# Sums over partitions and the spreading of 1/rms in the layer norms: two fp32r parts instead of float32

## The chip, the cores and the metric

The kernel runs on one core of a Trainium2 chip. The core has five engines that work side by side, each through its own queue in order: TensorE (PE, matrix products; PEld is its weight load), VectorE (DVE), ScalarE (ACT), GpSimd (POOL) and SyncE (SP, which issues the DMAs). The metric is the device time of one execution in microseconds (us). The kernel before took 1206.88 us, the median of three runs from 1206.43 to 1207.32.

## The reference

The program is a decoder trunk of two layers for one sequence of 512 tokens with 1024 features. What matters here is that each layer has three RMS norms over the features, and that every one feeds a matrix product:

```python
def rms_norm(x, g):
    y = x * lax.rsqrt(jnp.mean(x * x, axis=-1, keepdims=True) + EPS)
    return y * g
for l in range(DEPTH):
    hn = rms_norm(h, g_mix[l]);  proj = hn @ w_in[l]
    # causal differential attention (4 heads) and a gated recurrent block on proj
    h = h + jnp.concatenate([o, y], axis=-1) @ w_out[l]
    hm = rms_norm(h, g_mlp[l]);  h = h + jnp.square(jax.nn.relu(hm @ w_mlp_in[l])) @ w_mlp_out[l]
    gate = jax.nn.sigmoid(rms_norm(h, g_ple[l]) @ w_ple_gate[l])
    h = h + gate * (p[l] @ w_ple_proj[l])
return rms_norm(h, g_final)
```

## The kernel before

**Layout.** Features lie on the 128 partitions, tokens along the free dimension: `h` is eight tiles of 128x512. A product of a weight chunk (`wh`, `wl`) with activations (`hgh`, `hgl`, or `ffh`, `ffl`) fills an accumulator of 128x512. Each factor is cut into two fp32r parts, a rounded one (`...h`, ScalarE copy) and the rest (`...l`, VectorE subtraction); `split` (L506) does both. Each product then is three fp32r products (`mm3`, L511): high by high, high by low, low by high.

**Norms.** Nothing waits for 1/rms before a product: the weights are applied to `h` times the gain, and the accumulator is multiplied by 1/rms afterwards. `Norm.tile` (L671 on) squares each tile of `h` on ScalarE and adds it to `acc` on VectorE. `Norm.stats` (L692) sums `acc` over the partitions on TensorE: for each of four blocks of 128 tokens one float32 product with a column of 1/1024 (`onesd`), into `msq`, so that the tokens now lie on the partitions; then `me` (VectorE adds epsilon) and `rT` (GpSimd takes the power -1/2; at the feed-forward norm, which needs 1/ms, VectorE takes a reciprocal). `Norm.spread` (L706) brings it back with four float32 products: the stationary factor is a column of `rT`, repeated 128 times, and the moving one the identity (`ident`), into `bc`; ScalarE copies that to `rbc`. Everything that reads `rbc` evicts an accumulator: `xp`, `grx` and the rotary factors `cr`, `sr` (mix norm), `dn` (feed-forward norm), `gt` (embedding norm). There are six such norms, mix, feed-forward and embedding in each of two layers. The norm at the end is a class of its own (`FinalNorm`), and the norm of the heads calls the free function `spread` (L710).

**Accumulators.** `PM` (L419) draws from a ring of six banks for `dense`, `pj`, `up`, `pv` and `sc`; a seventh accumulator waits until the first reader is done with its bank. `PS` has two banks, for `msq`, `bc` and the small ones.

**Embedding stage.** `ple` (L1183) takes two tiles of features at a time: `pj` (the embedding's projection, 2 x 6 products) and then two `dense` (the gate, 48 products). In the first call of a layer all but the last of eight parts are done ahead, then `stats` and `spread` are recorded, then the rest (`late=1`, `mid=ple_ready`, L1225). `gate_done` reads `dense` and `rbc` into `gt`. The mix norm stands in the same way between the parts of the first two `dense` groups of a layer (`norm_ready`, L852).

**Order.** Nothing is issued as it is recorded. A planner (`Plan.schedule`, L184) simulates all engines with a table of costs (`Plan.cost`, L105), picks the next instruction within a window of 600 and also assigns buffers; the instructions are then issued in its order. On TensorE it counts for a float32 product four times its columns and at least 4 x 128, and for an fp32r product its columns and at least 256 (L114).

Of the kernel before, what the change touches and what calls it, by code (L numbers as in the profile page):

```python
# [11 lines left out]
F32 = mybir.dt.float32  # L12
F32R = mybir.dt.float32r
I32 = mybir.dt.int32
AF = mybir.ActivationFunctionType
ALU = mybir.AluOpType
# [3 lines left out]
NT = S // 128  # L20
D = 1024
# [8 lines left out]
EPS = 1e-6  # L30
# [370 lines left out]
def build(ctx: ExitStack, tc: tile.TileContext, given, x, p, pos, w, vec, lamqk, out):  # L401
    rnc = tc.nc
    nc = Plan(rnc, WIN, ('raw', 'wh', 'wl'), given)
    act = nc.scalar.activation
    ve = nc.vector
    mm = nc.tensor.matmul

    const = ctx.enter_context(tc.tile_pool(name="const", bufs=1))
# [7 lines left out]
    def T(name, dt=F32, n=S):  # L416
        return nc.tile(tp, [128, n], dt, "t", TB, name)
# [4 lines left out]
    def PS(name):  # L422
        return nc.tile(pss, [128, S], F32, "ps", 2, name)

    def SM(name, n, dt=F32):
        return nc.tile(small, [128, n], dt, name, 4, name)
# [79 lines left out]
    def split(src, hi, lo):  # L506

        act(out=hi, in_=src, func=AF.Copy)
        ve.tensor_tensor(out=lo, in0=src, in1=hi.bitcast(F32), op=ALU.subtract)
# [12 lines left out]
    identr = const.tile([128, 128], F32R, name="identr")  # L522
    maskr = const.tile([128, 128], F32R, name="maskr")
    onesd = const.tile([128, 1], F32, name="onesd")
    onese = const.tile([128, 1], F32, name="onese")
    mhalf = const.tile([128, 16], F32, name="mhalf")
    hb = const.tile([128, DEPTH, 8], F32, name="hb")
# [22 lines left out]
    def const_setup():  # L550
        make_identity(rnc, ident)
        ve.tensor_copy(out=identr, in_=ident)
        mk = T("mk")[:, 0:128]
        make_causal_mask(rnc, mk, mask_val=-1e30)
        ve.tensor_copy(out=maskr, in_=mk)
        nc.gpsimd.memset(onesd, 1.0 / D)
        nc.gpsimd.memset(onese, 1.0 / 128)
        nc.gpsimd.memset(mhalf, -0.5)

# [111 lines left out]
    class Norm:  # L671
# [20 lines left out]
        def stats(self, square=False):  # L692

            ps = PS("msq")
            for j in range(NT):
                mm(ps[:, j:j + 1], lhsT=self.acc[:, j * 128:(j + 1) * 128], rhs=onesd, start=True, stop=True)
            me = SM("me", NT)
            ve.tensor_scalar(out=me, in0=ps[:, 0:NT], scalar1=EPS, scalar2=None, op0=ALU.add)
            r = SM("rT", NT)
            if square:  # L700
                ve.reciprocal(out=r, in_=me)
            else:
                nc.gpsimd.tensor_tensor(out=r, in0=me, in1=mhalf[:, 0:NT], op=ALU.pow)
            self.rT = r

        def spread(self):  # L706
            self.bc = T("rbc")
            spread(self.rT, 0, self.bc)

    def spread(r, c, dst):  # L710
        ps = PS("bc")
# [66 lines left out]
    def layer(l, h, nm, last):  # L778
# [227 lines left out]
        def head_out(hd):  # L1006
            o, r = ho.pop(hd)
            ps = spread(r, 0, None)
            ve.tensor_tensor(out=o, in0=o, in1=ps, op=ALU.mult)
            hi, lo = T("oh", F32R), T("ol", F32R)  # L1010
            split(o, hi, lo)
            yo[hd] = (hi, lo)
# [222 lines left out]
    with tc.manual_schedule():  # L1235
# [3 lines left out]
        posi = T("posi", I32)[:, 0:NT]  # L1239
        split(*halves[0])  # L1240
        const_setup()
        nm = Norm("g_mix", 0)
        h = []
        for m in range(KD):
            t = T("h")
# [24 lines left out]
def trunk(tc, x, p, pos, w, vec, lamqk, out):  # L1270
    import concourse.bacc as bacc
    nc = bacc.Bacc("TRN2", target_bir_lowering=False, num_devices=1)
    a = [nc.dram_tensor(f"a{i}", t.shape, t.dtype, kind="ExternalInput").ap() for i, t in enumerate((x, p, pos, w, vec, lamqk, out))]
    with tile.TileContext(nc) as t0:
        plan = build(t0, None, *a)
    build(tc, plan, x, p, pos, w, vec, lamqk, out)
# [64 lines left out]
```

## Time and profile before

| | us |
|---|---|
| median of three runs (range) | 1206.88 (1206.43 to 1207.32) |
| the profiled execution | 1207.2 |
| its span, first to last instruction | 1205.2 |
| TensorE busy | 1191.3 (99%) |
| VectorE busy | 947.6 (79%) |
| ScalarE busy | 664.3 (55%) |
| GpSimd busy | 19.8 (2%) |
| share of TensorE in the chain that ended last | 91% |

The profiled execution took 2.0 us more than its span. An engine's busy time is the union of its instructions' times. Since TensorE's products overlap each other, the record of one is longer than its share: the distance from the start of one to the start of the next is its real cost. TensorE's granted clock is 0.996 of full speed over the span. Most of the kernel's instructions carry the line of the helper that issues them (L182), so rows are told apart by the names of the tiles, written out<-in.

### The profile page before, as it was taken

To read this page: it belongs to the slowest core of one execution; us is meant where nothing else is said; L and a number is where in the kernel's file an instruction comes from. 1 tells how busy PE (TensorE), PEld (TensorE's weight loads), DVE (VectorE), ACT (ScalarE), POOL (GpSimd) and SP (SyncE) were. 2 spreads that over 40 slices of the span, in tenths; PEclk is the share of its full clock that TensorE was granted. 3 is DMA by queue.
4 is the path that set the end of the run, shared out by engine and by line. 5 is a ranking of instruction groups with operands and counts; after the bars stand their busy time and mean duration, and the time that the engine had idled before them with its cause. 6 is when DMAs were issued, how large, how long until landed. Compare 5 with 4: busy or idle time off the path is not lost.

```text
span 1205.2 us, 17677 instructions
## 1 busy us (share of the span) xinstructions
PE 1191.3 (99%) x6848; PEld 1048.2 (87%) x6848; DVE 947.6 (79%) x1642; ACT 664.3 (55%) x1084; POOL 19.8 (2%) x43
## 2 busy tenths in 40 slices
PE   9999999999999999999999999999999999999996
PEld 6888888988989989988888888899899898898896
DVE  9899989987777678575778999799786787776564
ACT  6878747643534535543458777476355254364352
POOL 1000000000000000000000000000000000000000
PEclk9999999999999999999999999999999999999998
DMA  6321132243333333332323212224332333343202
GB/s 238 105 70 53 36 123 88 88 144 101 106 106 90 103 105 109 101 106 89 104 71 106 69 36 70 88 88 134 95 106 88 105 106 106 93 125 98 88 1 70
DMA packets 34371, 114.71 MB, mean 95 GB/s; under 512 B 3952, under 2 KB 6000, under 8 KB 34288
## 3 DMA queue, kind: packets, MB, share of 16 engines
q1 hardware_dynamic: 34288, 113.59, 30.3%
q8 instruction: 54, 0.88, 0.3%
q14 instruction: 29, 0.24, 0.1%
HBM read 111.48 MB, written 2.10 MB: 94 GB/s over the span
## 4 chain that ended last, share of the span: by engine, by line
PE 91%; DVE 5%; ACT 2%; issue 0%; DMA 0%; SPq 0%; POOLq 0%; DVEq 0%; ACTq 0%
PE dense L182 54%; PE up L182 27%; PE pv L182 2%; PE pj L182 2%; PE sc L182 2%; PE bc L182 1%; PE av L182 1%; DVE qr L182 1%; PE tr L182 1%; PE msq L182 1%; DVE wl L182 1%; DVE q L182 1%; PE osm L182 0%; PE gates L182 0%; DMA h<-x 0%
## 5 line engine op out<-in xcount | busy, mean ns | idle before, releaser
L182 ACT ACTIVATE wh<-raw 128x1024 fp32r<-128x1024 f32 x204 | 214.3, 1057 | 278.0 <-PE dense L182 154.5
L182 DVE TENSOR_TENSOR wl<-raw,wh 128x1024 fp32r<-128x1024 f32 x204 | 247.7, 1219 | 22.4 <-ACT wh L182 21.9
L182 PE MATMUL dense<-ffh,wh 128*128 128x512 f32 x512 | 199.5, 390 | 0.0
L182 PE MATMUL dense<-ffl,wh 128*128 128x512 f32 x512 | 199.3, 389 | 0.0
L182 PE MATMUL dense<-ffh,wl 128*128 128x512 f32 x512 | 199.2, 389 | 0.0
L182 PE MATMUL dense<-hgl,wh 128*128 128x512 f32 (+1 forms) x400 | 151.7, 379 | 0.0
L182 PE MATMUL dense<-hgh,wh 128*128 128x512 f32 (+1 forms) x400 | 150.8, 377 | 0.0
L182 PE MATMUL dense<-hgh,wl 128*128 128x512 f32 (+1 forms) x400 | 150.6, 376 | 0.0
L182 PEld LDWEIGHTS dense<-ffh,wl 128*128 128x128 f32 x512 | 96.1, 188 | 20.0
L182 PEld LDWEIGHTS dense<-ffh,wh 128*128 128x128 f32 x512 | 96.2, 188 | 19.7
L182 PEld LDWEIGHTS dense<-ffl,wh 128*128 128x128 f32 x512 | 96.2, 188 | 19.6
L182 DVE TENSOR_TENSOR dn<-dense,rbc 128x512 f32<-128x512 f32 x64 | 44.2, 691 | 73.5 <-PE dense L182 72.6
L182 PE MATMUL up<-bl,wh 128*128 128x256 f32 x352 | 99.6, 283 | 0.0
L182 PE MATMUL up<-bh,wl 128*128 128x256 f32 x352 | 99.6, 283 | 0.0
L182 PE MATMUL up<-bh,wh 128*128 128x256 f32 x352 | 99.5, 283 | 0.0
L182 ACT ACTIVATE sh<-s 128x512 fp32r<-128x512 f32 x96 | 60.0, 628 | 69.0 <-DVE s L182 68.2
L182 PEld LDWEIGHTS dense<-hgh,wh 128*128 128x128 f32 x400 | 75.5, 189 | 12.2
L182 PEld LDWEIGHTS dense<-hgl,wh 128*128 128x128 f32 x400 | 75.5, 189 | 11.9
L182 PEld LDWEIGHTS dense<-hgh,wl 128*128 128x128 f32 x400 | 75.5, 189 | 11.7
L182 PE MATMUL up<-bl,sh 128*128 128x256 f32 x288 | 81.5, 283 | 0.0
L182 PE MATMUL up<-bh,sl 128*128 128x256 f32 x288 | 81.5, 283 | 0.0
L182 PE MATMUL up<-bh,sh 128*128 128x256 f32 x288 | 81.4, 283 | 0.0
(237 smaller groups left out, 2576.5 us busy)
## 6 DMA issues: line engine op xcount, KB each, us to landing
raw<-w SPq DMA_DIRECT2D x204, 512.0 KB, 3.6
h<-x SPq DMA_DIRECT2D x8, 256.0 KB, 5.6
out<-fin SPq DMA_DIRECT2D x8, 256.0 KB, 2.4
w<-w SPq DMA_DIRECT2D x4, 256.0 KB, 4.5
pT<-p SPq DMA_DIRECT2D x4, 256.0 KB, 3.9
lq<-lamqk SPq DMA_DIRECT2D x1, 256.0 KB, 6.9
vt<-vec SPq DMA_DIRECT2D x1, 61.0 KB, 2.4
posi<-pos SPq DMA_DIRECT2D x1, 2.0 KB, 3.6
```

Of the source, the lines that this page charges most:

```text
L182: d["fn"](*d["args"], **d["kw"])
```

## The change

In `stats`, `acc` is split into two fp32r parts, `ach` (ScalarE) and `acl` (VectorE), and the four float32 products become eight fp32r products with two equal columns of 1/1024 (`onesr`); `me` reads every second column. In `Norm.spread`, `rT` is split on VectorE into `rh` (a cast) and `rl` (a subtraction), and the four float32 products become eight fp32r products with `identr`, an fp32r identity that the kernel already had. The final norm and the norm of the heads stay in float32.

```diff
--- before.py
+++ after.py
@@ -522,6 +522,7 @@
     identr = const.tile([128, 128], F32R, name="identr")
     maskr = const.tile([128, 128], F32R, name="maskr")
     onesd = const.tile([128, 1], F32, name="onesd")
+    onesr = const.tile([128, 2], F32R, name="onesr")
     onese = const.tile([128, 1], F32, name="onese")
     mhalf = const.tile([128, 16], F32, name="mhalf")
     hb = const.tile([128, DEPTH, 8], F32, name="hb")
@@ -554,6 +555,7 @@
         make_causal_mask(rnc, mk, mask_val=-1e30)
         ve.tensor_copy(out=maskr, in_=mk)
         nc.gpsimd.memset(onesd, 1.0 / D)
+        nc.gpsimd.memset(onesr.bitcast(F32), 1.0 / D)
         nc.gpsimd.memset(onese, 1.0 / 128)
         nc.gpsimd.memset(mhalf, -0.5)
 
@@ -692,10 +694,14 @@
         def stats(self, square=False):
 
             ps = PS("msq")
+            hi, lo = T("ach", F32R), T("acl", F32R)
+            split(self.acc, hi, lo)
             for j in range(NT):
-                mm(ps[:, j:j + 1], lhsT=self.acc[:, j * 128:(j + 1) * 128], rhs=onesd, start=True, stop=True)
+                ts = slice(j * 128, (j + 1) * 128)
+                mm(ps[:, 2 * j:2 * j + 2], lhsT=hi[:, ts], rhs=onesr, start=True, stop=False)
+                mm(ps[:, 2 * j:2 * j + 2], lhsT=lo[:, ts], rhs=onesr, start=False, stop=True)
             me = SM("me", NT)
-            ve.tensor_scalar(out=me, in0=ps[:, 0:NT], scalar1=EPS, scalar2=None, op0=ALU.add)
+            ve.tensor_scalar(out=me, in0=ps[:, 0:2 * NT].rearrange("p (j t) -> p j t", t=2)[:, :, 0], scalar1=EPS, scalar2=None, op0=ALU.add)
             r = SM("rT", NT)
             if square:
                 ve.reciprocal(out=r, in_=me)
@@ -705,7 +711,15 @@
 
         def spread(self):
             self.bc = T("rbc")
-            spread(self.rT, 0, self.bc)
+            rh, rl = SM("rh", NT, F32R), SM("rl", NT, F32R)
+            ve.tensor_copy(out=rh, in_=self.rT)
+            ve.tensor_tensor(out=rl, in0=self.rT, in1=rh.bitcast(F32), op=ALU.subtract)
+            ps = PS("bc")
+            for j in range(NT):
+                for r in (rh, rl):
+                    mm(ps[:, j * 128:(j + 1) * 128], lhsT=r[:, j:j + 1].to_broadcast([128, 128]), rhs=identr,
+                       start=r is rh, stop=r is rl)
+            act(out=self.bc, in_=ps, func=AF.Copy)
 
     def spread(r, c, dst):
         ps = PS("bc")
```

The planner then makes another order. Apart from tiles' numbers, TensorE's queue differs in layer 0 between its mix norm and the end of its attention, and from there on only within some fifty products around each norm.

TensorE, embedding norm of layer 0, before: the spreading (one row, four float32 products), ten products of the second pair's `pj`, and the first `dense` of that pair.

```order
L182 MATMUL bc_1254<-ident_77,rT_1252 128x128 x4
L182 MATMUL pj_1269<-pTh_1232,wl_1216 128x512
L182 MATMUL pj_1269<-pTh_1235,wh_1215 128x512
L182 MATMUL pj_1269<-pTl_1236,wh_1215 128x512
L182 MATMUL pj_1269<-pTh_1235,wl_1216 128x512
L182 MATMUL pj_1270<-pTh_1232,wh_1215 128x512
L182 MATMUL pj_1270<-pTl_1233,wh_1215 128x512
L182 MATMUL pj_1270<-pTh_1232,wl_1216 128x512
L182 MATMUL pj_1270<-pTh_1235,wh_1215 128x512
L182 MATMUL pj_1270<-pTl_1236,wh_1215 128x512
L182 MATMUL pj_1270<-pTh_1235,wl_1216 128x512
L182 MATMUL dense_1271<-hgh_1176,wh_1240 128x512
```

TensorE, the same place now, up to the same first `dense`; one `rh` product of the spreading stands six `pj` products further up.

```order
L182 MATMUL pj_1283<-pTh_1241,wl_1225 128x512
L182 MATMUL bc_1267<-identr_78,rl_1266 128x128
L182 MATMUL bc_1267<-identr_78,rh_1265 128x128
L182 MATMUL bc_1267<-identr_78,rl_1266 128x128
L182 MATMUL bc_1267<-identr_78,rh_1265 128x128
L182 MATMUL bc_1267<-identr_78,rl_1266 128x128
L182 MATMUL bc_1267<-identr_78,rh_1265 128x128
L182 MATMUL bc_1267<-identr_78,rl_1266 128x128
L182 MATMUL pj_1283<-pTh_1244,wh_1224 128x512
L182 MATMUL pj_1283<-pTl_1245,wh_1224 128x512
L182 MATMUL pj_1283<-pTh_1244,wl_1225 128x512
L182 MATMUL dense_1284<-hgh_1185,wh_1249 128x512
```

The last part of the spreading moved behind seven of the ten `pj` products: three stand between it and `dense`, not ten.

VectorE at the same norm, as a difference (wl is a weight chunk's low part, `gt` the first reader of `rbc`):

```order
+L182 TENSOR_TENSOR acl<-acc,ach 128x512
 L182 TENSOR_SCALAR me<-msq 128x4
-L182 TENSOR_TENSOR wl<-raw,wh 128x1024 x2
+L182 CAST rh<-rT 128x4
+L182 TENSOR_TENSOR wl<-raw,wh 128x1024
+L182 TENSOR_TENSOR rl<-rT,rh 128x4
+L182 TENSOR_TENSOR wl<-raw,wh 128x1024
 L182 TENSOR_TENSOR gt<-dense,rbc 128x512 x2
```

`acl` stands ahead of `me`; `rh` waits for GpSimd's `rT` with a `wl` behind it, and `rl` stands between two `wl`.

VectorE at the mix norm of layer 0, before, from `me` to the first reader of `rbc` (`turn`, `rd` and `sp5` belong to the set-up of rotary angles and of the recurrent block's constants):

```order
L182 TENSOR_SCALAR me_188<-msq_187 128x4
L182 TENSOR_TENSOR turn_163<-turn_163,pr_159 128x64
L182 TENSOR_TENSOR sp5_175<-sp5_175,sp4_174 128x8
L182 TENSOR_TENSOR wl_213<-raw_181,wh_212 128x1024
L182 TENSOR_TENSOR turn_163<-turn_163,pr_159 128x64
L182 TENSOR_SCALAR sp5_175<-sp5_175 128x8
L182 TENSOR_TENSOR wl_215<-raw_184,wh_214 128x1024
L182 TENSOR_SCALAR rd_164<-turn_163 128x64
L182 TENSOR_TENSOR sp5_175<-sp5_175,sp4_174 128x8
L182 TENSOR_TENSOR wl_230<-raw_216,wh_229 128x1024
L182 TENSOR_TENSOR xp_192<-dense_185,rbc_190 128x512
```

VectorE at the same norm now, from `me` to `rl`; `acl` stands six rows further up, in the place that `me` had, and `xp` nine rows further down, behind two more `wl`:

```order
L182 TENSOR_SCALAR me_191<-msq_188 128x4
L182 TENSOR_SCALAR rd_165<-turn_164 128x64
L182 TENSOR_TENSOR sp5_176<-sp5_176,sp4_175 128x8
L182 TENSOR_TENSOR wl_220<-raw_185,wh_219 128x1024
L182 TENSOR_SCALAR rd_165<-rd_165 128x64
L182 TENSOR_SCALAR sp5_176<-sp5_176 128x8
L182 CAST rh_194<-rT_192 128x4
L182 TENSOR_TENSOR turn_164<-turn_164,rd_165 128x64
L182 TENSOR_TENSOR sp5_176<-sp5_176,sp3_174 128x8
L182 TENSOR_TENSOR rl_195<-rT_192,rh_194 128x4
```

`me` moved down by six rows, `rh` and `rl` came in between it and `xp`, and the queue's small set-up work moved up between them.

## Rows read from the trace of the kernel before

**Rows 1.** The page: busy us, share, instructions; and VectorE's busy tenths in 40 slices.

```profile
PE 1191.3 (99%) x6848; PEld 1048.2 (87%) x6848; DVE 947.6 (79%) x1642; ACT 664.3 (55%) x1084; POOL 19.8 (2%) x43
...
DVE  9899989987777678575778999799786787776564
```

**Rows 2.** The chain that ended last, in time: start us, length us, engine and work.

```profile
20.49 0.79 PE msq L182 x8
...
249.51 1.39 PE dense L182 x6
...
461.70 40.31 PE up L182 x336
502.01 43.55 PE dense L182 x192
```

**Rows 3.** TensorE's waits for scores: in total us, times, longest us.

```profile
PE sc L182 <- ACT pr L182: 0.9, 2, 0.7
PE sc L182 <- ACT ky L182: 0.8, 1, 0.8
```

**Rows 4.** Timeline, embedding norm of layer 0: start us, length us, engine, work, [idle before].

```profile
557.41 0.39 PE L182 MATMUL dense<-hgh,wl 128*128 128x512 f32 x1
...
557.64 0.95 PE L182 MATMUL msq<-onesd,acc 128*128 128x1 f32 x8
...
558.45 0.49 PE L182 MATMUL dense<-hgh,wh 128*128 128x512 f32 x1
...
558.62 0.16 DVE L182 TENSOR_SCALAR me<-msq 128x4 f32<-128x4 f32 x1 [9.20 <-PE msq L182]
558.77 0.40 PE L182 MATMUL dense<-hgl,wh 128*128 128x512 f32 x1
...
558.86 1.01 POOL L182 TENSOR_TENSOR rT<-me,mhalf 128x4 f32<-128x4 f32 x1 [386.48 <-DVE me L182]
...
560.35 2.36 DVE L182 TENSOR_TENSOR wl<-raw,wh 128x1024 fp32r<-128x1024 f32 x2 [1.56 <-ACT wh L182]
...
560.39 1.05 PE L182 MATMUL bc<-ident,rT 128*128 128x128 f32 x8
...
561.20 0.47 PE L182 MATMUL pj<-pTh,wl 128*128 128x512 f32 x1
...
561.48 0.60 ACT L182 ACTIVATE rbc<-bc 128x512 f32<-128x512 f32 x1 [0.23 <-PE bc L182]
...
562.62 1.28 DVE L182 TENSOR_TENSOR gt<-dense,rbc 128x512 f32<-128x512 f32 x2
...
563.58 0.40 PE L182 MATMUL dense<-hgh,wh 128*128 128x512 f32 x1
```

**Rows 5.** Timeline of TensorE in attention of layer 0, narrow fp32r products.

```profile
118.59 0.28 PE L182 MATMUL sc<-ky,qx 128*128 128x256 f32 x1
...
118.82 0.22 PE L182 MATMUL sc<-maskr,identr 128*128 128x128 f32 x1
118.89 0.45 PE L182 MATMUL dense<-hgh,wh 128*128 128x512 f32 x1
119.17 0.49 PE L182 MATMUL tr<-ident,pr 128*128 128x128 f32 x3
```

**Rows 6.** Groups by line and shape: busy us, mean ns | idle before us.

```profile
L182 DVE TENSOR_TENSOR xcl<-xc,xch 128x512 fp32r<-128x512 f32 x8 | 5.3, 684 | 1.1 <-ACT xch L182 1.1
...
L182 ACT ACTIVATE xch<-xc 128x512 fp32r<-128x512 f32 x8 | 4.9, 622 | 0.6 <-DVE xc L182 0.5
```

**Rows 7.** Timeline, mix norm of layer 0: VectorE and GpSimd.

```profile
28.55 0.16 DVE L182 TENSOR_SCALAR me<-msq 128x4 f32<-128x4 f32 x1
...
28.86 2.07 POOL L182 TENSOR_TENSOR rT<-me,mhalf 128x4 f32<-128x4 f32 x1 [25.46 <-DVE turn L182]
...
32.81 1.29 DVE L182 TENSOR_TENSOR xp<-dense,rbc 128x512 f32<-128x512 f32 x2
```

**Rows 8.** Timeline of VectorE, first reader of layer 0's feed-forward norm.

```profile
261.11 0.68 DVE L182 TENSOR_TENSOR dn<-dense,rbc 128x512 f32<-128x512 f32 x1
```

## The prediction

> **What bounds the kernel now.** I read the page's busy shares first, then the chain that ended last in order of time, then TensorE's waits, and last the timeline around each norm. TensorE is busy 99% of the span [rows 1]. Its own spacing shows what that means: 192 products of 512 columns take 43.55 us, 0.227 us each, and 336 of 256 columns take 40.31 us, 0.120 us each [rows 2]. Such stretches follow each other with nothing between them in the feed-forward and embedding stages. So an edit shows in the time if it changes what TensorE has to stream, or makes it stand still. The exception is attention of layer 0, from about 30 to 180 us, where VectorE is busy at nine tenths or more in most slices [rows 1] and TensorE now and then waits for scores; the two listed waits there and in layer 1 come to 1.7 us [rows 3].
>
> **TensorE's own work: nothing.** There are six norms of the kind that the diff touches (mix, feed-forward and embedding, in two layers; the final one is left alone). In each, four float32 products for the sums stand in the trace as eight records, and four for the spreading as eight. Afterwards there are eight plus eight products in fp32r, one record each: 96 narrow records before, 96 after. Their price before: from the last wide product ahead of the sums to the second one behind them is 558.77 - 557.41 = 1.36 us; less two wide pitches of 0.227 that leaves 0.906 us for eight, 0.113 each. The eight of the spreading stand from 560.39 to 561.20, the same 0.81 us as the sums' from 557.64 to 558.45 [rows 4], so 0.113 too, though they have 128 columns and the sums one. The number of columns does not set that price. For fp32r there is a narrow row: the mask product of 128 columns. From 118.59 to 119.17 us stand two of 256 columns, one mask product and one wide one: 0.58 - 2 x 0.120 - 0.227 = 0.113 us [rows 5]. Same price, so 16 x 0.113 = 1.8 us per norm before and after: 0 in sum. Two columns in fp32r are not in the trace. The bounds: 0.057 (half of a narrow record; then 96 x 0.056 = 5.4 us are gained), and 0.120 (the 256-column row; then 0.7 us lost). I take 0.113, the fp32r row with the nearest shape.
>
> The Trainium skill, "TensorE: Matmul & The Clock Gate", section "Weight-path perf modes", has a fast weight load that is on when 128 weights are loaded in a type other than FP32, about twice as fast where measured; the same table says that fp32 gains nothing from it. By its trigger the change would gain, by its width not. The row of the mask product, 0.113 us in fp32r as in float32, speaks for no gain here.
>
> **What each norm's chain gains in length.** Before: sums, `me` (VectorE 0.16), `rT` (GpSimd 1.01), spreading, `rbc` (ScalarE 0.60) [rows 4]. New ahead of the sums: `ach` on ScalarE, priced as `xch` 0.62, and `acl` on VectorE, as `xcl` 0.68 [rows 6]. New between `rT` and the spreading: `rh` and `rl` on VectorE, 128x4 each, like `me` 0.16 each. That is 1.6 us of work and three more handoffs of 0.1 to 0.2 us each (from the end of `me` at 558.78 to `rT` it is 0.08; from the end of the sums at 558.45 to `me` 0.17) [rows 4]: 1.9 to 2.2 us. As load it is nothing: ScalarE +3.7 us and VectorE +6.0 us over the span, where they are busy 55% and 79% [rows 1]. What counts is who stands still for the delay, and that differs by stage.
>
> **Embedding norms (two): +1.1 us each.** VectorE idles 9.20 us ahead of `me` [rows 4], so `ach` and `acl` are done long before TensorE comes to the sums, and the sums stay where they were. But the order now puts only three `pj` products between the last spreading product and the next `dense`, where ten stood. That `dense` needs a seventh accumulator of a ring of six (two `pj` and two `dense` of the first pair, two `pj` of the second): it can start only when `gt` has read the first `dense`. Before, ten `pj` covered 561.20 to 563.58 = 2.38 us; `rbc` started 0.28 after 561.20, took 0.60, VectorE was held by two `wl` until 562.6, `gt` took 0.64, and TensorE went on at 563.58 [rows 4] with no gap. Needed without the `wl`: 0.28 + 0.60 + 0.64 and a handoff of 0.1 to 0.2 on either side of `gt`, 1.8 us. Left as cover: three `pj`, the first of which pays 0.32 like the product behind the sums, so 0.32 + 2 x 0.227 = 0.77. Short by 1.0 to 1.1 us; I take 1.1. Queued behind `rh` on VectorE are one `wl`, `rl` and another `wl`; `rl` comes at about 561.7 by the pair's 1.18 us each, and TensorE asks for it at 562.1, so that wait stays hidden. Bounds per norm: 0 if `gt` frees its bank in time, 2.0 if `gt` also queues behind a `wl`. The pattern is the same in both layers: 2.2 us.
>
> **Feed-forward norms (two): 0.** Here the order moves the sums past the end of the `up` products and the spreading 14 wide products behind the sums. `dense` began at 249.51 [rows 2] with the sums (0.9 us) ahead of it, so now at about 248.6; nine plus five plus fourteen wide products and sixteen narrow ones end at about 256.8, and `rbc` 0.9 later at 257.7. Its first reader `dn` started at 261.11 [rows 8], since it waits for its product. Some 3 us of cover remain. Bounds 0 and +0.5 (if `rl` comes late behind `ffl`).
>
> **Mix norm of layer 1: +0.3 us.** Fifteen wide products stand ahead of the last part of the spreading, instead of eight, so `xp` comes up to 7 x 0.227 = 1.6 us later. The first gate products stand 32 wide products behind the spreading instead of 35, so 0.9 us later in TensorE's queue. That is 0.7 us short; half of it I count as slack. Bounds 0 and 1.6.
>
> **Mix norm of layer 0: +1.0 us.** VectorE has no idle time here. `acl` takes the place in the queue where `me` stood at 28.55 [rows 7]; the first sum stands seven wide products behind 20.49, where the sums stood [rows 2], and the other seven 34 wide products further, so at 20.49 + 41 x 0.227 = 29.8 or a little later; `me` falls to 31, `rT` follows with 2.07 us as before, `rh` behind it holds VectorE's queue, and `xp` starts at about 35 instead of 32.81. TensorE has `pv` products to stream meanwhile. VectorE itself has 0.68 + 2 x 0.16 = 1.0 us more to do in a stretch in which it is nearly full. The order of layer 0's attention is also another one: the first scores stand earlier in TensorE's queue by some 3 us, their operands earlier on VectorE by less. The bounds: -1.7 (all waits for scores gone [rows 3]) and +3.1 (1.0 us of VectorE work and the 2.1 us of `rT` that now holds the queue, all of it TensorE's). I take +1.0, the work added to the full engine.
>
> **Sum:** 0 + 2.2 + 0 + 0.3 + 1.0 = +3.5 us. The profiled run took 1207.2 us with a span of 1205.2, so 1208.7 in the span and 1210.7 for the run. The median of the runs, 1206.88, lies 0.3 us under the profiled one: 1210.4 us.
>
> **Rivals.** *The cover holds.* The bank of the first `dense` comes free in time, as the DVE-to-TensorE handoff may be shorter and the `pj` slower, and layer 0 fills its gap with `pv`. For it: that VectorE is 79% busy and idles for 9 us ahead of `me`. Against it: seven `pj` of 0.227 less cover. Then only +0.8 us remains, 1207.7. *Layer 0 pays in full.* `rh` blocks VectorE behind the slow GpSimd `rT`, and scores come late for all four heads: 3.1 instead of 1.0 and 0.5 at one feed-forward norm: +6.1, 1213.0. For it the 9s of VectorE; against it the `pv` products, which wait for no norm. *Narrow fp32r passes are cheap* (the other side): at a price p per record the change gains 96 x (0.113 - p). It breaks even with +3.5 at p = 0.077, is faster by 0.2% at 0.051, and at 0.057 gives 1210.4 - 5.4 = 1205.0. For it: fp32r streams 256 columns at 0.120, the rate at which float32 takes 128 in two records. Against it: the mask row.
>
> This last rival is what the fast weight load of the Trainium skill's page named above would make of the time.
>
> **How the numbers follow.** 0.2% of 1206.9 is 2.4 us, about what a measurement of this kernel can tell from no change, so faster means under 1204.5 and slower over 1209.3. Forecast 0.50, of it 0.08 under 1209.3; cover holds 0.24, all of it within; layer 0 in full 0.16, slower; cheap passes 0.10, of it 0.06 faster. Slower 0.42 + 0.16 = 0.58, faster 0.06, same 0.36. The forecast's own range is 1208.5 to 1212.5; with the rivals until one fifth is left out, 1206.0 to 1214.0.
>
> **What would show it.** Right: eight sums in a row at the embedding norm still take 0.8 to 0.9 us; a gap of about 1 us on TensorE ahead of the first `dense` behind the last `pj`, released by VectorE's `gt`, in both layers; no gap in the feed-forward. Wrong: sums and spreading under 0.6 us for eight, or no gap there, or TensorE's waits in layer 0's attention changed by more than 3 us either way.

## The result, and the profile after

| | us |
|---|---|
| before, median of four runs (range) | 1206.66 (1206.31 to 1207.32) |
| after, median of four runs (range) | 1214.55 (1212.87 to 1215.72) |
| predicted | 1210.4 (1206.0 to 1214.0) |
| profiled execution after, its span | 1212.87, 1210.8 |

The ratio is 1.0064, with a 95% interval from 1.0051 to 1.0076. The kernel became slower, as forecast, but by 7.9 us instead of 3.5, and the time lies outside the range. The profiled execution is the fastest of the four, so the profiles can account for 5.7 of the 7.9 us (1212.87 less 1207.2).

TensorE's work did not change. On the page of the kernel after, the busy times answer to [rows 1]; the columns are the same.

```profile
PE 1191.9 (98%) x6848; PEld 1049.3 (87%) x6848; DVE 952.6 (79%) x1660; ACT 667.5 (55%) x1090; POOL 18.4 (2%) x44
```

TensorE is busy 1191.9 us instead of 1191.3, in a span 5.6 us longer, so 5.0 us more are spent standing still; time lost to a lower clock counts as busy. TensorE's waits answer to [rows 3]:

```profile
PE sc L182 <- ACT pr L182: 2.1, 3, 1.6
...
PE sc L182 <- ACT kl L182: 1.4, 1, 1.4
PE dense L182 <- DVE gt L182: 1.4, 2, 0.7
PE sc L182 <- ACT ky L182: 1.3, 2, 1.1
```

The waits for scores grew from 1.7 to 4.8 us; the prediction had named a change of more than 3 us there as a sign that it was wrong. The wait for `gt` is new.

The embedding norm of layer 0, to be laid beside [rows 4] (start us, length us, engine, work, [idle before]):

```profile
561.79 0.17 PE L182 MATMUL msq<-onesr,ach 128*128 128x2 f32 x1
...
562.60 0.48 PE L182 MATMUL dense<-hgh,wh 128*128 128x512 f32 x1
...
566.27 0.22 PE L182 MATMUL bc<-identr,rl 128*128 128x128 f32 x1
...
567.01 0.44 PE L182 MATMUL pj<-pTh,wh 128*128 128x512 f32 x1
...
567.21 0.60 ACT L182 ACTIVATE rbc<-bc 128x512 f32<-128x512 f32 x1 [1.80 <-PE bc L182]
...
567.51 0.40 PE L182 MATMUL pj<-pTh,wl 128*128 128x512 f32 x1
...
567.84 1.29 DVE L182 TENSOR_TENSOR gt<-dense,rbc 128x512 f32<-128x512 f32 x2 [0.92 <-ACT rbc L182]
...
568.58 0.50 PE L182 MATMUL dense<-hgh,wh 128*128 128x512 f32 x1 [0.68 <-DVE gt L182]
```

Eight sums take from 561.79 to 562.60, 0.81 us, and seven products of the spreading from 566.27 to 567.01, 0.74 us: 0.10 to 0.11 us each, as in float32. Then three `pj` products stand where ten stood, the last starts at 567.51 and would let the next product start at 567.74; `dense` starts at 568.58, released by `gt`. The wait is the forecast one.

Layer 0's attention in stretches, before and then after (TensorE busy, its weight load, VectorE, ScalarE, GpSimd busy, each with its number of instructions; then granted clock, DMA share, GB/s):

```profile
60.00:66.00 6.00, 6.00 (x28) 4.99 (x27) 6.00 (x8) 6.00 (x9) 0.00 (x0) 1.00 0.00 1
...
80.00:84.00 4.00, 3.19 (x18) 2.34 (x16) 3.94 (x7) 3.49 (x6) 0.00 (x0) 1.00 0.43 130
...
92.00:100.00 8.00, 8.00 (x40) 6.60 (x39) 7.76 (x21) 7.82 (x17) 0.00 (x0) 1.00 0.42 131
```

The same stretches after, and the one from 84 to 88 us:

```profile
60.00:66.00 6.00, 6.00 (x28) 4.99 (x27) 3.68 (x6) 5.95 (x9) 0.00 (x0) 1.00 0.00 0
...
80.00:84.00 4.00, 1.92 (x9) 1.60 (x10) 3.94 (x6) 3.88 (x6) 0.00 (x0) 0.88 0.00 0
84.00:88.00 4.00, 4.00 (x16) 3.29 (x16) 4.00 (x11) 0.56 (x1) 0.00 (x0) 0.69 0.65 230
92.00:100.00 8.00, 6.38 (x30) 5.17 (x30) 7.73 (x17) 7.00 (x16) 0.00 (x0) 1.00 0.36 96
```

Read down the columns. From 60 to 66 us TensorE loses nothing in either, but VectorE, full before, is idle for 2.3 us after. From 80 to 84 us TensorE is busy 1.92 us instead of 3.19. From 84 to 88 us it is "busy" all the time, but at a granted clock of 0.69. From 92 to 100 us it stands still again. TensorE's own rows of that stretch:

```profile
80.50 0.50 PE L182 MATMUL sc<-ky,qx 128*128 128x128 f32 x2 [1.08 <-ACT ky L182]
...
82.88 0.33 PE L182 MATMUL sc<-kl,qx 128*128 128x128 f32 x1 [1.41 <-ACT kl L182]
...
84.08 0.73 PE L182 MATMUL dense<-hgh,wl 128*128 128x512 f32 x1
84.61 0.63 PE L182 MATMUL dense<-hgh,wh 128*128 128x512 f32 x1
85.04 0.63 PE L182 MATMUL dense<-hgl,wh 128*128 128x512 f32 x1
...
86.63 0.40 PE L182 MATMUL dense<-hgh,wl 128*128 128x512 f32 x1
...
93.81 0.44 PE L182 MATMUL sc<-ky,qx 128*128 128x384 f32 x1 [1.62 <-ACT pr L182]
```

Three waits, 1.08 for `ky`, 1.41 for `kl`, 1.62 for `pr`, and between them wide products 0.43 us apart instead of 0.227. In the prediction's terms this is the step "mix norm of layer 0: +1.0". The same place before, TensorE's first score of `ky`, ScalarE's `kl`, and TensorE's first score of `kl`:

```profile
81.75 0.67 PE L182 MATMUL sc<-ky,qx 128*128 128x128 f32 x3 [0.81 <-ACT ky L182]
...
82.72 1.35 ACT L182 ACTIVATE kl<-kl 64x512 fp32r<-64x512 f32 x2 [0.36 <-DVE kl L182]
...
83.78 0.22 PE L182 MATMUL sc<-kl,qx 128*128 128x128 f32 x1
```

Before, 342 products stand ahead of the first score of `kl`, seven of them wide ones between the scores of `ky` and of `kl` (7 x 0.227 = 1.6 us). In the changed kernel 327 stand ahead, and no wide one in between. ScalarE begins `kl` 0.5 us sooner than before (82.20, in its rows further down, instead of 82.72). So the operand does not come later: TensorE asks for it sooner, and the cover is gone, as at the embedding norms.

For the comparisons below I worked out from the records how long TensorE stood still or ran slow up to a given time: the start of a product, less a full-speed pitch for every product ahead of it (0.227, 0.173, 0.120 and 0.108 us for 512, 384, 256 and at most 128 columns). The table gives what a kernel's profiled execution lost more than that of before, in two stretches and around the two embedding norms, and the difference of the medians within one comparison.

| kernel | 50 to 95 us | 95 to 180 us | embedding norms | medians | ratio, 95% interval |
|---|---|---|---|---|---|
| after | +6.3 | -1.9 | +1.0, +0.9 | +7.9 | 1.0051 to 1.0076 |
| e1 two parts in layer 0's mix norm only | +5.9 | -2.0 | 0.0, 0.0 | +4.9 | 1.0028 to 1.0053 |
| e2 in the five others only | 0.0 | -0.2 | +1.0, +1.0 | +2.2 | 1.0007 to 1.0025 |
| e3 all, old order | 0.0 | -0.1 | 0.0, 0.0 | +1.4 | 0.9999 to 1.0017 |
| e8 all, old order, split later | 0.0 | -0.2 | 0.0, 0.0 | 0.0 | 0.9991 to 1.0009 |
| e4 float32, window 580 | 0.0 | -0.7 | 0.0, 0.0 | -0.6 | 0.9985 to 1.0003 |
| e5 all, table constant 2.5 | +2.9 | +4.7 | +1.0, +0.9 | +8.1 | 1.0057 to 1.0082 |
| e14 all, window 560 | +5.8 | -1.2 | +1.0, +0.9 | +7.5 | 1.0047 to 1.0072 |
| e15 all, table constant 10 | 0.0 | -0.2 | +1.0, +0.9 | +2.6 | 1.0010 to 1.0028 |
| e7 after, two table loads fewer | +5.3 | -2.0 | +1.0, +0.9 | +5.5 | 1.0041 to 1.0068 |
| e9 after, less VectorE work | +4.9 | -2.0 | +1.0, +0.9 | +5.9 | 1.0033 to 1.0059 |
| e13 after, both | +3.3 | -2.0 | +1.0, +1.0 | +4.2 | 1.0020 to 1.0044 |
| e6 before, two table loads more | +3.0 | -0.4 | 0.0, 0.0 | +2.4 | 1.0012 to 1.0031 |
| e10 before, VectorE work at 69 us | +2.0 | 0.0 | 0.0, 0.0 | +4.5 | 1.0021 to 1.0047 |
| e11 before, the same at 30 us | 0.0 | 0.0 | 0.0, 0.0 | +0.8 | 0.9997 to 1.0015 |
| e12 old order, fewer narrow products | 0.0 | -0.1 | +0.3, +0.4 | -0.6 | 0.9985 to 1.0002 |
| e16 the same, feed-forward norms only | 0.0 | -0.2 | 0.0, 0.0 | -2.9 | 0.9968 to 0.9987 |

The -1.9 from 95 to 180 us is time that before loses there itself and the other order does not: from 120 to 150 us TensorE is busy 29.3 of 30 us before, 30.0 after. Outside these stretches no profile of a kernel with the change differs from before's by more than 0.4 us, except e12 (+0.7 at each feed-forward norm), the first 50 us, where they scatter from -0.6 to +1.1 (e3 +1.7), and the last 20 us, where before's profile loses up to 1.0 us more than theirs.

### The profile page after: what moved, and what is told of

Read it like the earlier page. It is cut to its first block, busy times and chain, and to the rows that moved or that the text cites. A ratio compares the mean times of both kernels' runs of the same rounds, so it can differ in the third digit from the quotient of the medians.

```text
span 1210.8 us, 17703 instructions
## 1 busy us (share of the span) xinstructions
PE 1191.9 (98%) x6848; PEld 1049.3 (87%) x6848; DVE 952.6 (79%) x1660; ACT 667.5 (55%) x1090; POOL 18.4 (2%) x44
## 4 chain that ended last, share of the span: by engine, by line
PE 90%; DVE 4%; ACT 4%; DMA 1%; issue 1%; SPq 0%; POOL 0%; POOLq 0%; DVEq 0%; ACTq 0%
PE dense L182 53%; PE up L182 27%; PE pv L182 3%; PE pj L182 2%; PE sc L182 2%; PE av L182 1%; PE bc L182 1%; ACT L182 1%; PE tr L182 1%; DVE wl L182 1%; PE gates L182 1%; ACT pr L182 0%; PE msq L182 0%; ACT a L182 0%; DMA raw<-w 0%
```

## Experiments: in which norm, and is it work or order

The first kernel makes the two parts in one norm, the second in the other five:

```diff
 class Norm:
+    self.two = g == "g_mix" and l == 0        # e1; in e2: not (...)
 def stats(self, square=False):
+    if self.two: ...two parts...  else: ...float32...
```

**e1.**

> Two parts only in the mix norm of layer 0; the other five norms stay in float32. Up to about 180 us the order is then the one of the changed kernel, behind it the one of before. The changed kernel lost 7.9 us by its median; in its profile TensorE lost 4.2 us more than before between 75 and 180 us and 1.0 us at each embedding norm. If the excess over the forecast lies in layer 0, as I hold: +4.2 to +6 us over before, with waits of TensorE for kl and for pr near 81 and 94 us and a lower granted clock behind them, and no wait of dense for gt. If it lay in the sum of many small costs over all six norms (rival): at most +2.

**e2.**

> Two parts in five norms; the mix norm of layer 0 stays in float32, and with it the order up to 180 us is the one of before. If the excess lies in layer 0: +2.0 us over before (two waits of dense for gt of about 1.0 each), nothing in the two feed-forward norms and in the mix norm of layer 1. Rival, costs spread over all norms: +5 or more.

Measured +4.9 and +2.2, together 7.1 of the 7.9. e2 shows the forecast's two embedding norms (2.2) to a tenth, and nothing else. e1 has nearly the whole excess (+4.9 where +1.0 was forecast), and in the same place as the changed kernel. The many-small-costs rival falls.

For the next the planner runs on the float32 program, and the new instructions are put into its order by hand:

```diff
 def issue(self):
-    for i in self.given.order:
+    old = self.given                      # plan of the float32 program
+    place(last + 1, k, "split")           # behind the last write of acc
+    place(later(sums, 24), k, "sums")     # k = 0: 24 TensorE products later
+    place(later(bc, 5), k, "bc")          # k = 0: 5 products later
+    ...
```

**e3.**

> The whole change, all six norms, but the planner runs on the float32 program: every other instruction keeps before's order and buffers, and the new ones are put in by hand, ach and acl right behind the last addition into acc, the sums and the spreading near their old places (in the mix norm of layer 0 the sums 24 and the spreading 5 products later, in the feed-forward norms 24 and 20, elsewhere 0 and 1). Theory A, the order makes the cost: the added work and links are hidden and the time is before's +0 to +1.5 us. Theory B, the added 1.0 us of VectorE work and the longer chain in the full layer 0 make it: +4 or more, with layer 0 alone losing at least 3.

**e8.**

> As the kernel in before's order, with ach and acl of layer 0's mix norm 14 TensorE products later, behind the weight part wl that they had held up (TensorE waited 1.4 us for it at 21 us, VectorE 0.7 us for ach). If that wait was all that the change still cost in the old order: before's time within 0.7 us. If the added work costs something of its own: still +1 or more.

e3 came out at +1.4, hardly to be told from no change; in its profile all of it lies before 25 us. VectorE's timeline of e3 there:

```profile
21.00 0.69 DVE L243 TENSOR_TENSOR acl<-acc,ach 128x512 fp32r<-128x512 f32 x1 [0.70 <-ACT ach L243]
21.61 1.22 DVE L243 TENSOR_TENSOR wl<-raw,wh 128x1024 fp32r<-128x1024 f32 x1
```

TensorE's timeline of e3, the product that waits:

```profile
22.89 0.50 PE L243 MATMUL dense<-hgh,wl 128*128 128x512 f32 x1 [1.38 <-DVE wl L243]
```

`acl` waited 0.70 us for ScalarE's `ach` with a `wl` behind it, and TensorE waited 1.38 us for that `wl`. With the split 14 products later (e8) the whole change costs 0.0, with an interval from 0.9991 to 1.0009, that is 1.1 us either way. Within that, neither the sixteen fp32r products nor 1.0 us of VectorE work nor the longer chain has a price of its own, in layer 0 or at the embedding norms. What costs is the order that the planner makes around them.

But not any other order. **e4** changes one number in the kernel before (`-WIN = 600`, `+WIN = 580`).

> The kernel before, float32, with the planner's window at 580 instead of 600: not an operation more or less, but another order of layer 0's attention up to about 180 us, and the same one behind it. Theory A, layer 0's time hangs on the order by several us: the time differs from before's by 2 us or more, either way. Theory B, the order as such is worth little: within 1 us of before.

It was within 1 us (-0.6). The expectation from the order theory, "2 us or more, either way", was wrong as put: some orders are as good as the old one.

## Experiments: what in that order costs the time

In this kernel ScalarE loads a table when it goes over from exponentials and tanh to a square root, and back: the whole kernel has 13 loads before and 13 after; e6 below adds two with an exponential behind a square root, and e7 takes away two by making square roots exponentials. The loads between 50 and 70 us, before and after:

```profile
50.70 1.28 ACT L182 ACT_TABLE_LOAD   x1
...
56.62 1.28 ACT L182 ACT_TABLE_LOAD   x1
...
66.23 1.28 ACT L182 ACT_TABLE_LOAD   x1
```

After, in the same stretch:

```profile
51.53 1.28 ACT L182 ACT_TABLE_LOAD   x1
...
54.24 1.28 ACT L182 ACT_TABLE_LOAD   x1
...
56.69 1.28 ACT L182 ACT_TABLE_LOAD   x1
...
62.42 1.28 ACT L182 ACT_TABLE_LOAD   x1
...
65.83 1.28 ACT L182 ACT_TABLE_LOAD   x1
```

Two more in this stretch, 1.28 us each, while ScalarE is full (5.95 of 6 us in the row from 60 to 66 above) and VectorE waits for it. VectorE's waits from 20 to 100 us, before and after:

```profile
DVE a L182 <- ACT tr L182: 2.1, 1, 2.1
```

After:

```profile
DVE a L182 <- ACT a L182: 2.2, 3, 1.3
DVE qx L182 <- ACT qx L182: 1.2, 1, 1.2
```

Between 20 and 80 us VectorE idles 4.7 us after, 3.4 before, with 1.0 us more to do. That made theory C, the loads. Three kernels tested it: e5, the planner's constant (`-SW = 2`, `+SW = 2.5`), e6 and e7:

```diff
+# e6: kernel before, behind the second square root of layer 0
+    scalar.activation(out=dmy, in_=mhalf[:, 0:1], func=AF.Exp)
+# e7: kernel after, first two square roots
+    d["kw"]["func"] = AF.Exp
```

**e5.**

> The whole change, with the planner's constant for changing ScalarE's table at 2.5 instead of 2. The order differs from the changed kernel's in layer 0 alone. Up to the first softmax it has 7 table loads, as before; the changed kernel has 9, and the two more (1.28 us each) stand in a stretch from 50 to 66 us in which ScalarE is busy all the time and VectorE waits for it. Theory C, the two loads make layer 0's loss: layer 0 loses at most 1 us, the time is before's +2 to +3 (the two embedding norms). Theory V, the added work on VectorE and the order of its queue make it: +6 or more, as the changed kernel.

**e6.**

> The kernel before, in its own order, with one exponential of 128x1 more behind the second square root of layer 0's gates. Its result is not used; it makes ScalarE load its table twice more, near 58 us. Theory C: VectorE falls behind by 1 to 2.5 us, TensorE stands still for the scores near 80 us, and the time rises by 2 to 5 us. Theory V: ScalarE has slack from 75 us on and takes the 2.6 us in; within 1 us of before.

**e7.**

> The changed kernel in its own order, with the first two square roots of layer 0's gates issued as exponentials, so that two of the nine table loads are not needed (two of the recurrence's factors are other numbers by this; everything else is computed as it was). Theory C: layer 0's loss of 4 to 5 us falls to 2 or less, the time to before's +2.5 to +4.5. Theory V: no change against the changed kernel, +7 to +8 over before.

The time of e6 agrees with C (+2.4), but not the way: `ky` is not among its TensorE waits, and the wait that is new is for `xch`, which ends at 63.9 us, with a granted clock of 0.86 behind it (66 to 75 us):

```profile
PE gates L183 <- ACT xch L183: 2.1, 1, 2.1
```

e7 falls between (+5.5: less than the changed kernel, more than C's 2.5 to 4.5), and e5 speaks against C: seven loads like before, and as slow as the changed kernel. (Its layer 0 loses 7.6 us in the table, but that profile is the slowest of five executions, and its longest wait is another one, 3.3 us for `pr`.) Two loads have a price there, but they are not the whole. Next, VectorE's lateness; like e7, e9 leaves a part of the computation out and serves for the time alone:

```diff
+# e9: kernel after, layer 0, token blocks 1 to 3; the products read vh for vl
+    n = 1
-    ve.scalar_tensor_tensor(out=lo, ...)
+    ve.scalar_tensor_tensor(out=lo[:, 0:n], ...)
+# e10, e11: kernel before, at 69 us and at 30 us
+    for _ in range(3): vector.tensor_tensor(out=dmy, in0=zz, in1=zz, op=ALU.subtract)
```

**e9.**

> The changed kernel in its own order, with three of layer 0's four vl (the low part of the values, 128x512 each, at 76.6, 78.5 and 80.3 us) cut to one column; the products read vh in their place, so that three quarters of layer 0's values lose their low part. That takes 1.8 us of work from VectorE just ahead of kl. Theory L, VectorE is about 2.3 us late at kl (1.3 us more idle than before up to 80 us, 1.0 us of added work) and TensorE's waits follow from that: the waits for ky and kl near 80 us fall under 1 us and the time by 2 to 4 us against the changed kernel. Theory T, the place of the first scores in TensorE's queue, eight products earlier than before, makes them: within 1 us of the changed kernel.

**e10.**

> The kernel before, in its own order, with three subtractions of 128x512 more on VectorE near 69 us, whose result is not used: 1.8 us of work in a stretch in which VectorE does not idle until 95 us. Theory L: TensorE waits for the first scores 1.5 to 2 us longer, +1.5 to +4 us. Theory T: +0.7 at most.

**e11.**

> The same three subtractions near 30 us, where the change has acl, rh and rl: ahead of the 2.1 us that VectorE idles at 51 us. If that idle time takes up work that is added ahead of it, within 0.7 us of before, though VectorE shows nine tenths and more there. If the work passes on through xp, xc and the gates to ScalarE's tr, for which that idle time waits: +1.5 or more.

e10 and e11 show that the same 1.8 us of VectorE work costs 2.0 us in the profile and 4.5 by the medians (at most 4 was expected) at 69 us, and 0.8, not to be told from no change, at 30 us. At 69 us nothing takes it up until TensorE stands still; at 30 us VectorE's idle time does: of the 3.4 us that it idles between 20 and 80 us before, 2.2 are left in e11, and 2.8 in e8. "VectorE has no idle time here" was wrong. e9 was a half miss. The time fell by about 2 us, but the waits for `ky` and `kl` did not move; what went is the wait for `pr` (2.1 to 0.7 us) behind them. ScalarE tells why the first two stayed. Its rows in the kernel after:

```profile
75.76 1.28 ACT L182 ACT_TABLE_LOAD   x1
...
77.59 1.04 ACT L182 ACTIVATE wh<-raw 128x1024 fp32r<-128x1024 f32 x1
78.54 2.56 ACT L182 ACTIVATE ky<-q 64x512 fp32r<-64x512 f32 x4
81.12 1.06 ACT L182 ACTIVATE wh<-raw 128x1024 fp32r<-128x1024 f32 x1
82.20 1.28 ACT L182 ACTIVATE kl<-kl 64x512 fp32r<-64x512 f32 x2
...
88.67 1.06 ACT L182 ACTIVATE wh<-raw 128x1024 fp32r<-128x1024 f32 x1 [4.11 <-DMA raw<-w]
```

`ky` stands behind a table load and a `wh`, `kl` behind another `wh`; and the next `wh` but one waited 4.11 us for a DMA. The DMA share is 0.00 from 80 to 84 us in the row above, where two `wl`, whose reading frees the buffers, stood behind `kl` on VectorE. So two engines are late, and each stands behind the other.

**e13**, both cuts.

> The changed kernel in its own order with both cuts at once: two square roots of layer 0's gates issued as exponentials (two table loads fewer on ScalarE) and three of layer 0's vl cut to one column (1.8 us of VectorE fewer); factors of the recurrence and the low part of layer 0's values are other numbers by this. Each cut alone left +5.6 and +5.9 us over before. If both engines are late and each hides the other: layer 0's loss goes nearly, +2 to +3.5 over before (the two embedding norms are 2.1 of it). If the order leaves TensorE without weight parts whatever those two engines do: +4.5 or more.

+4.2, between the two answers. By the table, layer 0 loses net 4.4 us in the changed kernel (50 to 180 us), 3.2 with two loads fewer, 2.9 with less VectorE work, and 1.3 with both: so the cuts give 1.1 and 1.5 alone and 3.1 together, by one profile each. They about add up; that each hides the other, as I had thought, is not so. (By the medians they give 2.4 and 2.0 alone and 3.7 together; the intervals of e7 and e9 still overlap the changed kernel's, that of e13 does not.) What is left in e13, 3.3 us up to 95 us less 2.0 gained later, is the wait for `kl`, here in TensorE's waits, and the clock behind it:

```profile
PE sc L187 <- ACT kl L187: 1.4, 1, 1.4
```

The stretch behind it, columns as above:

```profile
84.00:88.00 4.00, 4.00 (x15) 3.18 (x15) 4.00 (x9) 1.69 (x3) 0.00 (x0) 0.69 0.69 248
```

Two more orders of the changed program, by one number each (e14 `WIN = 560`, e15 `SW = 10`), chosen by what can be counted in an order: table loads up to the first softmax, and `wl` on VectorE ahead of the first `kl`.

**e14.**

> The whole change, planner's window 560 instead of 600: another order of layer 0, from the second half of the first heads on, that like the changed kernel's has 9 table loads up to the first softmax and 10 low weight parts wl on VectorE ahead of the first kl. If these two make the loss: +6 to +9 over before. If the loss came from the later part of layer 0's order or from chance: +4 or less.

**e15.**

> The whole change, planner's constant for changing the table at 10 instead of 2: 6 table loads up to the first softmax, 14 wl ahead of the first kl, the first scores 20 products later in TensorE's queue. If weight parts done ahead and few loads are what counts: layer 0 loses at most 1 us, +1 to +3.5 over before by the embedding norms. If this order is late elsewhere: +5 or more.

Both as expected: +7.5 with 9 loads and 10 `wl`, +2.6 with 6 and 14, of which 1.9 us are the embedding norms. Over all the orders run, with nothing added to them, those with 12 `wl` or more lose nothing in layer 0 (before, e2, e3, e4, e8, e15) and those with 10 lose 4 to 8 us (after, e1, e5, e14), while the loads (7 in e5) do not sort them. That the count of `wl` is the cause was not tried by itself, so it stays a sign and not a cause. The cover ahead of `kl` sorts them just as well: the first score of `kl` stands 10 or 13 products behind the first of `ky` in the former, 2 or 3 in the latter. No kernel here moves the one without the other, and in e5 the longest wait is not at `kl`. The Trainium skill, "ScalarE: Activation LUTs", section "Table sets: the hidden batching unit", advises to group calls by table set. e15 follows that furthest of all (6 loads) and is the best of the planner's four orders of the changed program; e5 (7 loads, +8.1) shows that it does not suffice here.

## Experiments: a version that is faster

A narrow product costs 0.10 to 0.11 us in both types, with 1, 2 or 128 columns. So the change saves nothing, but fewer products would.

```diff
+# feed-forward norms (e12, e16): no spreading
+    mm(ps, lhsT=onesw, rhs=ach, start=True, stop=False)   # onesw: 128x128 of 1/1024
+    mm(ps, lhsT=onesw, rhs=acl, start=False, stop=True)   # 512 columns each
+    ve.tensor_scalar(out=rbc, in0=ps, scalar1=EPS, op0=ALU.add)
+    ve.reciprocal(out=rbc, in_=rbc)
+# embedding norms (e12 only): ach, acl = identity times rh, rl
+    mm(ps, lhsT=onesw, rhs=ach, ...); mm(ps, lhsT=onesw, rhs=acl, ...)
```

**e12.**

> A version to beat both. Before's order with the change, as in the kernel with the late split, but fewer narrow products, since one costs 0.113 us whatever its shape. Feed-forward norms: ach and acl as the moving factor of two products of 512 columns with a stationary 1/1024 in 128 columns give the mean in all rows at once, VectorE takes 1/x of 128x512, and the spreading falls away (0.45 us of TensorE instead of 1.81). Embedding norms: the sums 12 products earlier, rh and rl times the identity (two VectorE products of 128x512) spread by two products of 512 columns (0.45 instead of 0.91). Mix norms as in the change. If TensorE's saved time shows: 2 x 1.36 + 2 x 0.45 = 3.6 us less, 1203. If VectorE's longer work (4 us for each 1/x) or a late rbc takes it back: 1206 or more.

**e16.**

> As the version with fewer narrow products, but only the two feed-forward norms are made so (sums by two products of 512 columns, 1/x of 128x512 on VectorE, no spreading); the embedding norms are as in the change. The 3.3 us of 1/x now stand behind the two ffl that they had held up, where VectorE idles 2.5 us for a DMA. If TensorE's 1.36 us per norm stay saved: 2.7 us under before, 1204. If dn or the weight parts behind it come late: 1206 or more.

e12 gave most of it back (-0.6, not to be told from no change). The reciprocal of 128x512 took 3.34 us and stood ahead of two `ffl`, for which TensorE waited, 0.7 us lost at each feed-forward norm; at the embedding norms `gt` became the bound again, 0.3 to 0.4 us each. Some more lies outside the span: an execution of e12 took 2.2 to 3.2 us more than its span, before's 2.0 to 2.1. e16 leaves those alone and puts the reciprocal behind the `ffl`. Its feed-forward norm of layer 0:

```profile
246.96 0.39 PE L246 MATMUL msq<-ach,onesw 128*128 128x512 f32 x1
...
247.19 0.39 PE L246 MATMUL msq<-acl,onesw 128*128 128x512 f32 x1
...
248.41 0.68 DVE L246 TENSOR_SCALAR rbc<-msq 128x512 f32<-128x512 f32 x1
...
255.05 3.35 DVE L246 RECIPROCAL rbc<-rbc 128x512 f32<-128x512 f32 x1
...
261.56 0.68 DVE L246 TENSOR_TENSOR dn<-dense,rbc 128x512 f32<-128x512 f32 x1
```

Two products in 0.45 us replace sixteen in 1.81. `dn`, the first reader, starts long after the reciprocal's end at 258.40. The time is 1203.56 us, 2.9 under before (interval 0.9968 to 0.9987), where 2 x 1.36 = 2.7 were expected. This version beats both.

## Why the prediction was right or wrong

- **TensorE's own work, 0: right.** 0.10 to 0.11 us per record in fp32r with 2 and with 128 columns. "Cheap passes" is dead. With it falls what the fast weight load of the Trainium skill's page "TensorE: Matmul & The Clock Gate", section "Weight-path perf modes", would have made of the time: the same 0.81 us for eight records in both types shows no gain.
- **Embedding norms, +1.1 each: right.** +1.0 and +0.9 in every kernel with this order (after, e2 and others), for the reason given: three `pj` as cover and `gt` late. In the old order, with the cover back, 0 (e8). "The cover holds" is dead.
- **Feed-forward norms 0: right**, within 0.1. **Mix norm of layer 1, +0.3: a little too much.** No profile lost 0.1 us more than before's there, so its lower bound came true.
- **Mix norm of layer 0, +1.0: this step failed.** The term was sized by the work added to VectorE, and its upper bound by that and the 2.1 us of `rT`. Both were the wrong thing to price. The added work costs nothing that can be told from 0 when it is put into the old order (e8) or ahead of VectorE's idle time (e11). The cost, 4.4 us in the profile (6.3 lost up to 95 us, 1.9 gained later) and 4.9 by e1's median, comes from what the planner did with the rest of layer 0 (e1, e3, e8, e15). Two more table loads on ScalarE are 1.1 us of it (e7) and VectorE's work ahead of the scores 1.5 (e9). The largest part, 3.3 us up to 95 us, stays when both are cut (e13): the wait for `kl` and the lower clock behind it, for which the prediction had no term. That the missing cover makes this part is read from the rows and not shown by an experiment. I had noted that "the order of layer 0's attention is also another one" by some 3 us in TensorE's queue and by less on VectorE, and then priced that only as a gain (the bound of -1.7); in the rows TensorE waits there for `ky` and `kl` instead. The rival "layer 0 pays in full" had the right sign with the wrong cause, and was 1.6 us short.
- **The sum.** The terms outside layer 0 gave +2.5 and came out at about +2.2 (e2). The rest of the miss, +7.9 by medians against +5.7 between the profiled executions, lies between executions of the same kernel: the profiled one is the fastest, the slowest took 2.9 us more. No trace shows where. The mean granted clock of the changed kernel's runs is 0.990 to 0.994, so a lower clock may be part of it.

## What to carry to other kernels

Where a planner orders the program, price the new order, not only the added instructions: count on each engine what the order itself shows (table loads, weight parts done ahead of a first use, products left as cover), in the stretch where two engines are full. A full engine with idle gaps ahead, as VectorE in e10 and e11, takes up work put before them and passes on work put behind them. And where narrow products cost the same in every type, change their number, not their type.

## What was not expected of the hardware

After waits, TensorE's granted clock fell to 0.69 from 84 to 88 us (0.88 in the stretch ahead), that is partly at the lower of its two levels (1.2 instead of 2.4 GHz). Six wide products took from 84.08 to 86.63 us, 2.55 instead of 1.36; the waits ahead of it (1.08, 0.17 and 1.41 us between 79.2 and 82.9) come to 2.7 us. In e6's profile the clock fell behind one wait of 2.1 us (its row above). One wait of 2.8 us did not do it in e10's profile, as its waits show:

```profile
PE sc L183 <- ACT ky L183: 2.8, 1, 2.8
```

The stretch behind that wait:

```profile
84.00:88.00 4.00, 4.00 (x23) 3.44 (x24) 3.94 (x7) 2.79 (x4) 0.00 (x0) 1.00 0.53 135
```

The clock stayed at 1.00 and the loss was 2.0 us. But that execution is the fastest of its five by 2.1 us (1208.70 against 1210.84 to 1212.29), and its mean clock is 0.997 against 0.993 to 0.995. So the same wait seems to draw the lower clock in most executions and not in some; which of them, no trace here shows.

VectorE's reciprocal of 128x512 took 3.35 us, against 0.68 for adding a constant to a tile of that size (rows of e16 above).
